# A ConvFFN down projection on one core: operand rests only on VectorE, in source order, with three more operand slots and paired steps

## The chip, the core and the metric

The kernel runs on one core of one Trainium2 chip. The metric is the device time of one execution in microseconds (us). TensorE (PE) does the matrix products, VectorE (DVE), ScalarE (ACT) and GpSimd (POOL) prepare operands and take results out of the banks, SyncE (SP) issues most transfers.

## What is computed

One layer of a hybrid block on 1024 tokens of width 1024: norm, three mixers, a residual, then a ConvFFN and a last norm. The change lies in the ConvFFN's last product; hidden width is 2816 = 22 x 128.

```python
def conv_ffn(u, w_up, conv_w, conv_b, w_down):
    hid = dwconv(u @ w_up, conv_w, conv_b, (1, 1))
    gate, val = jnp.split(hid, 2, axis=-1)
    return (jax.nn.silu(gate) * val) @ w_down
...
    h = h + mod[5] * conv_ffn(u, ffn_w_up[l], ffn_conv_w[l], ffn_conv_b[l], ffn_w_down[l])
  return rms_norm(h, final_g)
```

## The kernel before, in words

**Precision.** Every fp32 operand of a product is split into a rounded part and a rest (`split`, L214): ScalarE casts the source (L215), then the rest = source - rounded part is subtracted (L216), on VectorE or on GpSimd as the argument `lo` says. Three matmuls (high x high, low x high, high x low) make one product.

**Up projection (before L1927).** 22 pairs of blocks (gate and value) are made one after the other. `Pair.conv` (L1680) convolves one of the two along the tokens, `Pair.out` (L1701) convolves both, multiplies silu(gate) by the value and writes 512 KB to a buffer in HBM (`hid[i]`). The convolution of the last pair, i = 21, falls into the down projection.

**Down projection (L1927 to L2190).** A Strassen-like scheme with 2 x 2 blocks and seven products, run as four parts, each over 11 slices k of the hidden width (`K2 = 11`; slice k pairs the blocks k and k + 11):

- the alpha part (loop at L2091): two products, into four banks X and four banks Y. Its operands for slice k are two blocks of the weight (`wr`, one load of 512 KB per slice) and two of the hidden values (`hd`, two loads of 512 KB), made by `alpha_ops` (L2018). The sums of hidden blocks that the later parts need are made here by `sums_b` (L2022), three VectorE subtractions per slice, three slices behind (`LAG`).
- the beta part (L2114): its operands need more subtractions (`beta_ops`, L2032: L2035, L2037, L2039, and L2042 for the gamma part).
- the gamma part (L2129), and the delta part (L2175), whose operands are all made ahead.

A step (`step`, L1987) is one slice into one group of four banks: 4 x 3 = 12 matmuls of 128 x 512, at L1991 (high x high; the first argument is the stationary block), L1992 (its rest) and L1993 (the other operand's rest). Up to now every slice is one X step, then one Y step. Between two parts `add_to` (L1995, L1998) adds the banks to the residual on VectorE, four instructions per group.

**Operand slots.** An operand takes a slot of 128 x 1024 (`operand`, L1976). There are three with the tag `wh`, three with `wl`, and from the 13th operand on (`GV_AT = 12`) four with `gv`: 10 in all. A slot is free when the step that read its operand is done.

**Order.** PE's order is that of the source throughout. From L1927 to L2079 (`turn_order`) the other engines keep to the source too; behind L2079 a list scheduler orders VectorE, ScalarE and GpSimd by its own estimates. SP issues the loads in a queue: a `wr` load stands until one of two buffers is free, that is until both rests of the slice two before are done.

Of the kernel before, what the change touches and what calls it, by code (L numbers as in the profile page):

```python
# [9 lines left out]
F32R = mybir.dt.float32r  # L10
# [13 lines left out]
HID = 22  # L24
LAG = 3
LAG1 = 2
OUT_AT = 1
GV_AT = 12
HT_AT = 7
UP_DVE = (1, 4, 6)  # L30
# [78 lines left out]


def tile_kernel(tc, I, out, dbg=None):
    nc = tc.nc
    V, S, G, PE, SY = nc.vector, nc.scalar, nc.gpsimd, nc.tensor, nc.sync
    es = ExitStack()
    left = dict(side="left")
    right = dict(side="right")

    cst = es.enter_context(tc.tile_pool(name="cst", bufs=1, **left))
    wst = es.enter_context(tc.tile_pool(name="wst", bufs=1, **left))
# [6 lines left out]
    def nm(s):  # L126
        cnt[0] += 1
        return f"{s}{cnt[0]}"
# [4 lines left out]
    def t4(name="x", dt=F32):  # L133
        return px_.tile([128, 1024], dt, name=nm(name), tag="x", bufs=8)
# [4 lines left out]
    def pt(shape=(128, 512), dt=F32):  # L139
        return wst.tile(list(shape), dt, name=nm("pt"), tag="pt", bufs=2)  # L140
# [73 lines left out]
    def split(h, l, src, lo=G):  # L214
        S.copy(h, src)  # L215
        lo.tensor_tensor(l, src, f32(h), OP.subtract)  # L216
# [1331 lines left out]
    for m in range(KT):  # L1548
        w = wm.pop(0)
        p = mm()  # L1550
        tg = wide_in(tsp[m], "tg")
        for k in range(4):
            kk = slice(k * 128, (k + 1) * 128)
# [15 lines left out]
    pgv_ = pgv.__enter__()  # L1569
# [36 lines left out]
    def product(bk, w, b, first, ks=range(4)):  # L1606
        for k in ks:
            product_k(bk, w, b, first, k)

    class Pair:  # L1610
# [69 lines left out]
        def conv(self, b):  # L1680
# [17 lines left out]
                                       a[:, t0_ + c - 1:t0_ + n - 1], OP.mult, OP.add)  # L1698
            return a

        def out(self, queue=SY):  # L1701
            ga, va = self.conv(0), self.conv(1)
            S.activation(ga, ga, AF.Silu)
            V.tensor_tensor(ga, ga, va, OP.mult)
            queue.dma_start(hid[self.i], ga)

    q = [Pair(0), Pair(1)]
    accs = []
    for j in range(2):
        sl = tl[j]  # L1710
        acc = pt()
        for m in range(8):
            w = wm.pop(0)
# [3 lines left out]
            for k in range(KT):  # L1717
                kk = slice(k * 128, (k + 1) * 128)
# [40 lines left out]
    def bank(tag):  # L1759
        return pu_.tile([128, 512], F32, name=nm("bk" + tag), tag="bk" + tag, bufs=2)  # L1760
# [128 lines left out]
    norm_order.__exit__(None, None, None)  # L1889
    nxt.sums((7, 3))  # L1890
    q[0].p4()
    q[0].out()
    q[1].p3()
    q[1].p4()
    nxt.open("cd")
    for i in range(2, HID):
        pair, nxt = nxt, None
        if i > 2:
            pair.p1()
        pair.c1()  # L1900
        pair.load(5)
        if i > 2:
            pair.open()
            pair.p6()
        pair.z6()
        pair.load(7)
        product(pair.C, pair.w[5], T1, True)
        pair.load(2)
        product(pair.D, pair.w[7], T3, True)
        pair.z57()  # L1910
        pair.load(3, 4)
        if i + 1 == HID:
            break
        pair.p2()
        nxt = Pair(i + 1)
        nxt.fetch()
        nxt.sums()
        pair.p3()
        nxt.load(1, 6)
        if i == 2:  # L1920
            q[1].out()
        pair.p4()
        pair.out()

    turn_order = tc.manual_schedule(engines=ENGS - {mybir.EngineType.SP})  # L1927
# [10 lines left out]
    K2 = HID // 2  # L1938
    pdl = tc.tile_pool(name="pdl", bufs=1, **left, reuse_waits="tile")
    pdr = tc.tile_pool(name="pdr", bufs=1, **right, reuse_waits="tile")  # L1940
    pd = pdl.__enter__(), pdr.__enter__()
    home = {}
    for n in range(16):
        home["l", n] = 0
# [25 lines left out]
    def hid_load(k, queue=SY):  # L1970
        for i in (k, k + K2):
            queue.dma_start(raw[i], hid[i])

    ops_n = [0]

    def operand(src, lo=V):  # L1976

        c = ops_n[0] % 10 if ops_n[0] >= GV_AT else ops_n[0] % 2
        if c in (2, 5, 8, 9):
            w = pgv_.tile([128, 1024], F32R, name=nm("wp"), tag="gv", bufs=4)  # L1980
        else:
            w = wst.tile([128, 1024], F32R, name=nm("wp"), tag=("wh", "wl")[c % 2], bufs=3)
        ops_n[0] += 1
        split(w[:, 0:512], w[:, 512:1024], src, lo)
        return w

    def step(acc, w, b, first=False):  # L1987
        for m in range(4):
            mw = slice(m * 128, (m + 1) * 128)
            wh, wl = w[:, 0:512][:, mw], w[:, 512:1024][:, mw]  # L1990
            PE.matmul(acc[m], wh, b[:, 0:512], start=first, stop=False, skip_group_check=True)  # L1991
            PE.matmul(acc[m], wl, b[:, 0:512], start=False, stop=False, skip_group_check=True)  # L1992
            PE.matmul(acc[m], wh, b[:, 512:1024], start=False, stop=True, skip_group_check=True)  # L1993

    def add_to(r, c, acc):  # L1995
        for m in range(4):
            x = hT[4 * r + m][:, tl[c]]
            V.scalar_tensor_tensor(x, acc[m], md5[:, 4 * r + m:4 * r + m + 1], x, OP.mult, OP.add)  # L1998

    def b11(k):  # L2000
        return raw[k][:, tl[0]]

    def b12(k):
        return raw[k][:, tl[1]]

    def b21(k):
        return raw[k + K2][:, tl[0]]

    def b22(k):
        return raw[k + K2][:, tl[1]]  # L2010
# [4 lines left out]
    def alpha_load(k):  # L2015
        aw[k] = wraw(wd[k][:, 0:1024])

    def alpha_ops(k):  # L2018
        a12, a11 = (aw[k][:, t] for t in tl)
        return operand(a11, G), operand(b11(k)), operand(a12, G), operand(b21(k))  # L2020

    def sums_b(k):  # L2022
        V.tensor_tensor(b11(k), b12(k), b11(k), OP.subtract)
        V.tensor_tensor(spare[k], b22(k), b11(k), OP.subtract)
        V.tensor_tensor(b21(k), b21(k), spare[k], OP.subtract)

    def beta_load(k):
        a11 = tmp()
        SY.dma_start(a11, wd[k][:, 512:1024])
        aw[k] = a11, wraw(wd[k][:, 1024:2048])  # L2030

    def beta_ops(k):  # L2032
        a11, r = aw[k]
        a21, a22 = r[:, tl[0]], r[:, tl[1]]
        V.tensor_tensor(a22, a21, a22, OP.add)  # L2035
        t1 = operand(b11(k))
        V.tensor_tensor(b11(k), a11, a21, OP.subtract)  # L2037
        t2 = operand(spare[k])
        V.tensor_tensor(spare[k], a22, a11, OP.subtract)  # L2039
        s2 = operand(spare[k])  # L2040
        s1 = operand(a22)
        V.tensor_tensor(b12(k), b22(k), b12(k), OP.subtract)  # L2042
        return s2, t2, s1, t1

    def gamma_load(k):
        aw[k] = tmp()
        SY.dma_start(aw[k], wd[k][:, 0:512])

    def gamma_ops(k):
        s3, t3 = operand(b11(k)), operand(b12(k))  # L2050
        V.tensor_tensor(aw[k], aw[k], spare[k], OP.subtract)
        return s3, t3, operand(aw[k]), operand(b22(k))
# [21 lines left out]
    ops = [alpha_ops(0)]  # L2074
    V.tensor_tensor(pair.gv[0][:, tl[1]], pair.gv[1][:, tl[1]], pair.C, OP.add)
    X = [bank(t) for t in "abcd"]
    V.tensor_tensor(pair.gv[1][:, tl[1]], pair.gv[1][:, tl[1]], pair.D, OP.add)
    ops.append(alpha_ops(1))
    turn_order.__exit__(None, None, None)  # L2079
    hid_load(2)  # L2080
    alpha_load(2)
    hT = []
# [1 line left out]
    def h_loads(n):  # L2084
        if 0 <= n - HT_AT < 8:
            hx = t4("h")
            SY.dma_start(hx, hsp[n - HT_AT])
            hT.append(hx)

    Y = [bank(t) for t in "abcd"]  # L2090
    for k in range(K2):  # L2091
        if k + 3 < K2:
            if k + 3 < K2 - 1:
                hid_load(k + 3)
            alpha_load(k + 3)
        w1, o1, w2, o2 = ops.pop(0)
        step(X, w1, o1, k == 0)
        step(Y, w2, o2, k == 0)
        if k == OUT_AT:
            pair.out(S)  # L2100
        if k == OUT_AT + 2:
            hid_load(K2 - 1)
        h_loads(k)
        if k + 2 < K2:
            ops.append(alpha_ops(k + 2))
        elif k + 2 == K2:
            beta_load(0)
        if k >= LAG:
            sums_b(k - LAG)
    add_to(0, 0, X)  # L2110
    beta_load(1)
    ops = [beta_ops(k) for k in range(2)]
    add_to(0, 0, Y)
    for k in range(K2):  # L2114
        if k + LAG1 < K2 and k + LAG1 > K2 - 1 - LAG:
            sums_b(k + LAG1)
        w1, o1, w2, o2 = ops.pop(0)
        step(X, w1, o1)
        step(Y, w2, o2, k == 0)
        h_loads(K2 + k)  # L2120
        if k + 2 < K2:
            beta_load(k + 2)
            ops.append(beta_ops(k + 2))
        else:
            gamma_load(k + 2 - K2)
    add_to(0, 1, X)
    add_to(1, 1, Y)
    ops = [gamma_ops(k) for k in range(2)]
    for k in range(K2):  # L2129
        w1, o1, w2, o2 = ops.pop(0)  # L2130
        step(X, w1, o1)
        step(Y, w2, o2)
        if k + 2 < K2:
            gamma_load(k + 2)
            ops.append(gamma_ops(k + 2))
        if k % 2 == 0:
            delta_load(k)
        delta_ops(k)
    add_to(1, 1, X)
    add_to(0, 1, Y)  # L2140

# [30 lines left out]
    for c0, c1 in ((0, 256), (256, 512)):  # L2172
        for m in range(4):
            mw = slice(m * 128, (m + 1) * 128)
            for k in range(K2):  # L2175
                wh, wl = (w[:, mw] for w in dw[k])
# [11 lines left out]
    c0, c1 = pend[1]  # L2188
    last_out(c0, c1, norm_sums(pend[0], (c1 - c0) // 128, bank("a")))
    pe_order.__exit__(None, None, None)  # L2190
    pdr.__exit__(None, None, None)
    pgv.__exit__(None, None, None)
    px.__exit__(None, None, None)
# [98 lines left out]
```

## Time and profile before

| | |
|---|---|
| three runs | 1617.78, 1621.47 (median), 1622.53 us |
| profiled execution | 1620.94 us, span of the records 1619.1 us |
| PE busy | 1527.9 us, 94% of the span |
| VectorE busy | 1095.1 us, 68% |
| ScalarE busy | 770.0 us, 48% |
| GpSimd busy | 504.8 us, 31% |
| granted TensorE clock | mean 0.978 of full |

The page shows PE busy for nine tenths of the span: time can be gained there only by closing PE's gaps. The shares are means over all stages, so the rows below are taken from the stretch of the down projection, some 1365 to 1575 us from the span's start. A busy time counts a matmul from its start to a modelled end, so that neighbours overlap; the pace is read from the starts.

### The profile page before, as it was taken

How to read it: one execution, taken by the hardware profiler on the slowest of the kernel's cores; microseconds unless marked ns; L12 is line 12 of the kernel's file. 1: busy time of each engine (PE TensorE's matmuls, PEld its weight loads, DVE VectorE, ACT ScalarE, POOL GpSimd, SP SyncE). 2: the span in 40 equal slices, each digit the busy share in tenths (PEclk: the TensorE clock that was granted, in tenths of full speed). 3: DMA queues.
4: the chain of work that ended last, by engine and by line, in shares of the span. 5: the costliest groups of instructions: out<-in, count | busy, mean ns of one | idle time of the engine just before them, and what ended most of it. 6: DMA issues, size and time to landing. Idle time of an engine off the chain costs nothing. (4 is left out here: it accounts for less than half of the span.)

```text
span 1619.1 us, 21583 instructions
## 1 busy us (share of the span) xinstructions
PE 1527.9 (94%) x8144; PEld 1256.8 (78%) x8144; DVE 1095.1 (68%) x1598; ACT 770.0 (48%) x1221; POOL 504.8 (31%) x313
## 2 busy tenths in 40 slices
PE   5999999799998999999999998999999999789997
PEld 4888767677887788788888767878888888568887
DVE  4533569979877442642451799888888887898962
ACT  4424776665545544441333555444444444334661
POOL 3313233421113332222236444333333333630032
PEclk9999999899999999999999999999999999999998
DMA  9663623222214245132574411222222225664203
GB/s 347 236 220 98 223 84 115 95 86 66 68 53 131 94 124 157 54 88 72 170 233 141 142 41 62 81 80 101 80 78 79 79 88 202 223 247 156 98 20 105
DMA packets 93784, 198.91 MB, mean 123 GB/s; under 512 B 13488, under 2 KB 34864, under 8 KB 93552
## 3 DMA queue, kind: packets, MB, share of 16 engines
q1 hardware_dynamic: 81968, 181.62, 33.6%
q10 hardware_dynamic: 11712, 15.91, 2.8%
q8 instruction: 64, 1.05, 0.3%
q14 instruction: 40, 0.33, 0.1%
HBM read 158.98 MB, written 38.52 MB: 122 GB/s over the span
## 5 line engine op out<-in xcount | busy, mean ns | idle before, releaser
L216 POOL TENSOR_TENSOR wl<-wr,wh 128x1024 fp32r<-128x1024 f32 (+2 forms) x87 | 183.3, 2109 | 455.5 <-ACT wh L215 428.2
L215 ACT CAST wh<-wr 128x1024 fp32r<-128x1024 f32 (+2 forms) x87 | 77.3, 891 | 140.4 <-issue 42.0
L216 POOL TENSOR_TENSOR wp<-tmp,wp 128x512 fp32r<-128x512 f32 x44 | 73.9, 1698 | 221.5 <-ACT wp L215 221.5
L529 PE MATMUL ma<-uh,wh 128*128 128x512 f32 x272 | 117.4, 432 | 4.5 <-ACT pt L796 4.5
L529 PE MATMUL mb<-uh,wh 128*128 128x512 f32 x272 | 107.0, 394 | 0.0
L531 PE MATMUL ma<-ul,wh 128*128 128x512 f32 x272 | 107.0, 393 | 0.0
L531 PE MATMUL mb<-ul,wh 128*128 128x512 f32 x272 | 106.9, 393 | 0.0
L533 PE MATMUL mb<-uh,wl 128*128 128x512 f32 x272 | 106.6, 392 | 0.0
L533 PE MATMUL ma<-uh,wl 128*128 128x512 f32 x272 | 106.4, 391 | 0.0
L216 POOL TENSOR_TENSOR wp<-wr,wp 128x512 fp32r<-128x512 f32 x44 | 82.1, 1878 | 40.5 <-ACT wp L215 40.5
L215 ACT CAST wp<-tmp 128x512 fp32r<-128x512 f32 x78 | 46.5, 620 | 96.1 <-DVE tmp L1630 92.2
L1694 DVE SCALAR_TENSOR_TENSOR ca<-gv,vec,ca 128x1023 f32<-128x1023 f32 (+2 forms) x66 | 62.3, 968 | 24.4 <-ACT ca L1686 24.2
L215 ACT CAST wp<-hd 128x512 fp32r<-128x512 f32 x88 | 51.7, 618 | 55.1 <-PE bkd L1993 39.9
L215 ACT CAST wp<-wr 128x512 fp32r<-128x512 f32 x97 | 57.4, 620 | 42.5 <-DVE wr L2035 9.7
L1697 DVE SCALAR_TENSOR_TENSOR ca<-gv,vec,ca 128x1023 f32<-128x1023 f32 (+2 forms) x66 | 73.1, 1131 | 0.0
L216 DVE TENSOR_TENSOR wp<-hd,wp 128x512 fp32r<-128x512 f32 x88 | 61.4, 723 | 13.8 <-ACT wp L215 13.5
L529 PEld LDWEIGHTS ma<-uh,wh 128*128 128x128 f32 x272 | 51.7, 190 | 20.9 <-issue 6.7
L533 PEld LDWEIGHTS ma<-uh,wl 128*128 128x128 f32 x272 | 51.4, 189 | 11.5
L533 PEld LDWEIGHTS mb<-uh,wl 128*128 128x128 f32 x272 | 51.3, 189 | 11.4
L531 PEld LDWEIGHTS ma<-ul,wh 128*128 128x128 f32 x272 | 51.3, 189 | 11.3
L531 PEld LDWEIGHTS mb<-ul,wh 128*128 128x128 f32 x272 | 51.3, 189 | 11.3
L529 PEld LDWEIGHTS mb<-uh,wh 128*128 128x128 f32 x272 | 51.7, 190 | 9.7 <-issue 1.4
(628 smaller groups left out, 4634.2 us busy)
## 6 DMA issues: line engine op xcount, KB each, us to landing
wa<-in_ada_dram SPq DMA_DIRECT2D x96, 256.0 KB
wr<-in_wup_dram SPq DMA_DIRECT2D x46, 512.0 KB
wr<-in_win_dram SPq DMA_DIRECT2D x40, 512.0 KB
wr<-in_wdn_dram SPq DMA_DIRECT2D x22, 512.0 KB
hd<-hid SPq DMA_DIRECT2D x22, 512.0 KB
hid<-ca SPq DMA_DIRECT2D x21, 512.0 KB
wr<-in_wout_dram SPq DMA_DIRECT2D x16, 512.0 KB
tmp<-in_wdn_dram SPq DMA_DIRECT2D x22, 256.0 KB
```

Of the source, the lines that this page charges most:

```text
L215: S.copy(h, src)
L216: lo.tensor_tensor(l, src, f32(h), OP.subtract)
L529: PE.matmul(p[j], h[:, kk], uh[j][:, k], start=f, stop=False)
L531: PE.matmul(p[j], h[:, kk], ul[j][:, k], start=False, stop=False)
L533: PE.matmul(p[j], l[:, kk], uh[j][:, k], start=False, stop=e)
L1694: V.scalar_tensor_tensor(a[:, t0_ + 1:t0_ + 1 + n1], x[:, o:o + n1], fw[0], a[:, t0_ + 1:t0_ + 1 + n1], OP.mult, OP.add)
L1697: V.scalar_tensor_tensor(a[:, t0_ + c - 1:t0_ + n - 1], x[:, o + c:o + n], fw[2], a[:, t0_ + c - 1:t0_ + n - 1], OP.mult, OP.add)
```

## The change

It does five things, all in the down projection:

- `alpha_ops` makes its two weight operands' rests on VectorE instead of GpSimd (22 instructions).
- `turn_order` ends in the round k = 8 of the alpha loop instead of ahead of it, so that the engines follow the source that far; in the loop `sums_b` now stands ahead of `alpha_ops`.
- `Pair.out` no longer convolves the gate; a new `Pair.gate` does. For the last pair, `gate` stands in the round k = 0 and `out` in k = 1. For all other pairs `gate` stands directly ahead of `out`, which leaves their instructions in the same order.
- a third tag, `wz`, with three slots: 9 slots from the start and 13 from the 13th operand on, taken in a fixed rotation.
- PE's steps: the first two and the last two slices of a part go X, X, Y, Y instead of X, Y, X, Y (`steps`).

```diff
 class Pair:
+        def gate(self):
+            self.ga = self.conv(0)
+
         def out(self, queue=SY):
-            ga, va = self.conv(0), self.conv(1)
+            ga, va = self.ga, self.conv(1)
...
     def operand(src, lo=V):
-        c = ops_n[0] % 10 if ops_n[0] >= GV_AT else ops_n[0] % 2
-        if c in (2, 5, 8, 9):
-            w = pgv_.tile([128, 1024], F32R, name=nm("wp"), tag="gv", bufs=4)
-        else:
-            w = wst.tile([128, 1024], F32R, name=nm("wp"), tag=("wh", "wl")[c % 2], bufs=3)
+        c = ops_n[0] - GV_AT
+        tag = ("wh", "wl", "wz", "gv")[min(c % 13 % 4 if c % 13 < 12 else 3, 3)] if c >= 0 else ("wh", "wl", "wz")[c % 3]
+        w = {"gv": pgv_, "wz": pd[2]}.get(tag, wst).tile([128, 1024], F32R, name=nm("wp"), tag=tag,
+                                                        bufs=4 if tag == "gv" else 3)
...
     def alpha_ops(k):
-        return operand(a11, G), operand(b11(k)), operand(a12, G), operand(b21(k))
+        return operand(a11), operand(b11(k)), operand(a12), operand(b21(k))
...
     ops.append(alpha_ops(1))
-    turn_order.__exit__(None, None, None)
...
+    def steps(k, first_x, first_y):
+        def do(acc, kk, first):
+            w1, o1, w2, o2 = ops[kk]
+            step(acc, *((w1, o1) if acc is X else (w2, o2)), first)
+        if k in (0, K2 - 2):
+            for acc, f in ((X, first_x), (Y, first_y)):
+                do(acc, k, f and k == 0)
+                do(acc, k + 1, False)
+        elif k not in (1, K2 - 1):
+            do(X, k, False)
+            do(Y, k, False)
...
     for k in range(K2):
...
-        w1, o1, w2, o2 = ops.pop(0)
-        step(X, w1, o1, k == 0)
-        step(Y, w2, o2, k == 0)
-        if k == OUT_AT:
+        steps(k, True, True)
+        if k == 0:
+            pair.gate()
+        if k == 1:
             pair.out(S)
-        if k == OUT_AT + 2:
+        if k == 3:
             hid_load(K2 - 1)
         h_loads(k)
+        if k >= LAG:
+            sums_b(k - LAG)
         if k + 2 < K2:
             ops.append(alpha_ops(k + 2))
         elif k + 2 == K2:
             beta_load(0)
-        if k >= LAG:
-            sums_b(k - LAG)
+        if k + 2 == K2 - 1:
+            turn_order.__exit__(None, None, None)
```

**VectorE at the start of the alpha part, before.** `wp` is an operand, `hd` a hidden block, `wr` a weight block, `ca` the last convolution; L216 is a rest, L2023 to L2025 the sums:

```order
L216 TENSOR_TENSOR wp_11249<-hd_11225,wp_11249 128x512
L2023 TENSOR_TENSOR hd_11225<-hd_11225 128x512
L2024 TENSOR_TENSOR hd_11229<-hd_11226,hd_11225 128x512
L216 TENSOR_TENSOR wp_11255<-hd_11226,wp_11255 128x512
L2075 TENSOR_TENSOR gv_11102<-gv_11103,bkc_11109 128x512
L2025 TENSOR_TENSOR hd_11226<-hd_11226,hd_11229 128x512
L2077 TENSOR_TENSOR gv_11103<-gv_11103,bkd_11110 128x512
L216 TENSOR_TENSOR wp_11267<-hd_11235,wp_11267 128x512
L1694 SCALAR_TENSOR_TENSOR ca_11353<-gv_11102,vec,ca_11353 128x1023
L216 TENSOR_TENSOR wp_11273<-hd_11236,wp_11273 128x512
```

The same place in the changed kernel (a rest is now L215, and lines behind it are five further on):

```order
L215 TENSOR_TENSOR wp_11249<-wr_11243,wp_11249 128x512
L215 TENSOR_TENSOR wp_11252<-hd_11228,wp_11252 128x512
L215 TENSOR_TENSOR wp_11255<-wr_11243,wp_11255 128x512
L215 TENSOR_TENSOR wp_11258<-hd_11229,wp_11258 128x512
L2080 TENSOR_TENSOR gv_11102<-gv_11103,bkc_11109 128x512
L2082 TENSOR_TENSOR gv_11103<-gv_11103,bkd_11110 128x512
L215 TENSOR_TENSOR wp_11267<-wr_11247,wp_11267 128x512
L215 TENSOR_TENSOR wp_11270<-hd_11238,wp_11270 128x512
L215 TENSOR_TENSOR wp_11273<-wr_11247,wp_11273 128x512
L215 TENSOR_TENSOR wp_11276<-hd_11239,wp_11276 128x512
```

All four rests of a slice stand together, and the sums, which stood among them, come later: the first one stands 29 rows behind the first row shown here.

**GpSimd at the same place, before** (the first 5 of 22 such rows; the row ahead of them is the up projection's last):

```order
L216 TENSOR_TENSOR wp_11157<-pt_11041,wp_11157 128x512
L216 TENSOR_TENSOR wp_11246<-wr_11240,wp_11246 128x512
L216 TENSOR_TENSOR wp_11252<-wr_11240,wp_11252 128x512
L216 TENSOR_TENSOR wp_11264<-wr_11244,wp_11264 128x512
L216 TENSOR_TENSOR wp_11270<-wr_11244,wp_11270 128x512
```

And now, where what follows the up projection is the squares' sum of the last norm:

```order
L215 TENSOR_TENSOR wp_11139<-wr_11031,wp_11139 128x512
L215 TENSOR_TENSOR wp_11157<-pt_11041,wp_11157 128x512
L2178 TENSOR_TENSOR acc_12776<-acc_12776,tmp_12779 128x512
L2178 TENSOR_TENSOR acc_12776<-acc_12776,tmp_12783 128x512
L2178 TENSOR_TENSOR acc_12776<-acc_12776,tmp_12787 128x512
```

No GpSimd instruction is left between the up projection and the last norm.

**VectorE from the alpha part to the beta part, before** (`h` is the residual, `bka` to `bkd` the X banks; `wp_11756` is the weight operand of beta's first X step, `wp_11759` of its first Y step):

```order
L2035 TENSOR_TENSOR wr_11705<-wr_11705 128x512
L2037 TENSOR_TENSOR hd_11225<-tmp_11703,wr_11705 128x512
L2039 TENSOR_TENSOR hd_11229<-wr_11705,tmp_11703 128x512
L216 TENSOR_TENSOR wp_11759<-wr_11705,wp_11759 128x512
L1998 SCALAR_TENSOR_TENSOR h_11619<-bka_11259,md,h_11619 128x512
L1998 SCALAR_TENSOR_TENSOR h_11660<-bkb_11260,md,h_11660 128x512
L1998 SCALAR_TENSOR_TENSOR h_11701<-bkc_11261,md,h_11701 128x512
L1998 SCALAR_TENSOR_TENSOR h_11734<-bkd_11262,md,h_11734 128x512
L216 TENSOR_TENSOR wp_11756<-hd_11229,wp_11756 128x512
```

And now (numbers differ between the programs: `wp_11759` is here the weight operand of beta's first X step):

```order
L2040 TENSOR_TENSOR wr_11735<-wr_11735 128x512
L2003 SCALAR_TENSOR_TENSOR h_11621<-bka_11262,md,h_11621 128x512
L2003 SCALAR_TENSOR_TENSOR h_11662<-bkb_11263,md,h_11662 128x512
L2003 SCALAR_TENSOR_TENSOR h_11728<-bkc_11264,md,h_11728 128x512
L2003 SCALAR_TENSOR_TENSOR h_11737<-bkd_11265,md,h_11737 128x512
L2042 TENSOR_TENSOR hd_11228<-tmp_11733,wr_11735 128x512
L215 TENSOR_TENSOR wp_11755<-hd_11232,wp_11755 128x512
L215 TENSOR_TENSOR wp_11762<-wr_11735,wp_11762 128x512
L2044 TENSOR_TENSOR hd_11232<-wr_11735,tmp_11733 128x512
L2040 TENSOR_TENSOR wr_11748<-wr_11748 128x512
L215 TENSOR_TENSOR wp_11767<-hd_11238,wp_11767 128x512
L215 TENSOR_TENSOR wp_11759<-hd_11232,wp_11759 128x512
```

The four additions of the X banks now stand ahead of the subtractions (L2042, L2044) that beta's first X step needs.

## Rows read from the trace of the kernel before

**Rows 1.** Busy time by stage: alpha, beta, gamma, and beta and gamma without gaps.

```profile
core 0: us, PE busy (x) PEld busy (x) DVE busy (x) ACT busy (x) POOL busy (x), PEclk, DMA share, GB/s
1371.20:1445.60 74.40, 63.50 (x265) 50.46 (x264) 67.26 (x82) 28.36 (x49) 40.70 (x20) 0.95 0.67 242
...
1453.40:1571.40 118.00, 118.00 (x513) 96.04 (x513) 99.45 (x157) 64.52 (x113) 5.89 (x5) 1.00 0.30 99
```

**Rows 2.** Timeline of PE (start us, us; in brackets idle before and releaser).

```profile
1371.21 0.39 PE L1991 MATMUL bka<-wp,wp 128*128 128x512 f32 x1
...
1395.85 0.40 PE L1991 MATMUL bka<-wp,wp 128*128 128x512 f32 x1
...
1404.21 0.79 PE L1992 MATMUL bka<-wp,wp 128*128 128x512 f32 x1 [7.96 <-POOL wp L216]
1404.80 0.63 PE L1993 MATMUL bka<-wp,wp 128*128 128x512 f32 x1
...
1445.67 0.40 PE L1991 MATMUL bka<-wp,wp 128*128 128x512 f32 x1
1447.57 0.50 PE L1992 MATMUL bka<-wp,wp 128*128 128x512 f32 x1 [1.50 <-DVE wp L216]
...
1451.85 0.51 PE L1991 MATMUL bka<-wp,wp 128*128 128x512 f32 x1 [1.47 <-DVE h L1998]
...
1453.45 0.40 PE L1992 MATMUL bkb<-wp,wp 128*128 128x512 f32 x1
```

**Rows 3.** GpSimd: its rests in the alpha part, and its timeline at the longest.

```profile
L216 POOL TENSOR_TENSOR wp<-wr,wp 128x512 fp32r<-128x512 f32 x22 | 44.6, 2050 | 35.6 <-ACT wp L215 35.6
...
1391.92 15.94 POOL L216 TENSOR_TENSOR wp<-wr,wp 128x512 fp32r<-128x512 f32 x4 [4.43 <-ACT wp L215]
```

**Rows 4.** What SP's queue waited for, 1355 to 1480 us (us in total, times, longest).

```profile
SPq L206 <- POOL wp L216: 51.8, 10, 16.5
```

**Rows 5.** Transfers in stretches of 5 us, and over 1360 to 1440 us (columns as in rows 1).

```profile
1370.00:1375.00 5.00, 5.00 (x23) 4.12 (x23) 4.91 (x7) 1.44 (x3) 1.89 (x3) 1.00 1.03 415
...
1400.00:1405.00 5.00, 0.79 (x2) 0.70 (x3) 3.03 (x6) 0.00 (x0) 5.00 (x2) 0.62 0.00 0
...
DMA packets 5848, 21.37 MB, mean 267 GB/s; under 512 B 640, under 2 KB 640, under 8 KB 5844
```

**Rows 6.** Timeline of VectorE (first and last rows of stretches).

```profile
1368.04 0.88 DVE L216 TENSOR_TENSOR wp<-hd,wp 128x512 fp32r<-128x512 f32 x1 [3.43 <-ACT wp L215]
...
1384.57 1.78 DVE L2023 TENSOR_TENSOR hd<-hd 128x512 f32<-128x512 f32 x1
...
1390.31 0.68 DVE L2023 TENSOR_TENSOR hd<-hd 128x512 f32<-128x512 f32 x1
1390.91 0.68 DVE L2025 TENSOR_TENSOR hd<-hd,hd 128x512 f32<-128x512 f32 x1
...
1444.21 0.73 DVE L1998 SCALAR_TENSOR_TENSOR h<-bka,md,h 128x512 f32<-128x512 f32 x1
1444.87 0.73 DVE L1998 SCALAR_TENSOR_TENSOR h<-bkb,md,h 128x512 f32<-128x512 f32 x1
```

**Rows 7.** VectorE's groups with shapes: two of 1365 to 1440 us, then 1455 to 1500 us.

```profile
L2023 DVE TENSOR_TENSOR hd<-hd 128x512 f32<-128x512 f32 x11 | 11.7, 1070 | 0.1
L1697 DVE SCALAR_TENSOR_TENSOR ca<-gv,vec,ca 128x1023 f32<-128x1023 f32 x1 | 1.3, 1273 | 0.0
...
L216 DVE TENSOR_TENSOR wp<-hd,wp 128x512 fp32r<-128x512 f32 x27 | 17.8, 682 | 2.6 <-ACT wp L215 2.6
L216 DVE TENSOR_TENSOR wp<-wr,wp 128x512 fp32r<-128x512 f32 x9 | 6.2, 684 | 1.5 <-ACT wp L215 1.5
```

**Rows 8.** ScalarE's timeline: a cast, and the last pair's write on its queue.

```profile
1367.39 0.62 ACT L215 CAST wp<-hd 128x512 fp32r<-128x512 f32 x1 [0.40 <-DMA hd<-hid]
...
1389.81 0.33 ACTq L1705 DMA_DIRECT2D hid<-ca  x1
1390.18 1.14 ACT L215 CAST wp<-hd 128x512 fp32r<-128x512 f32 x2 [6.19 <-DVE ca L1704]
```

More of the change, by code (lines that the diff above doesn't have):

```diff
@@ L26 @@
 LAG1 = 2
-OUT_AT = 1
 GV_AT = 12
@@ L1891, in tile_kernel @@
     q[0].p4()
+    q[0].gate()
     q[0].out()
@@ L1920, in tile_kernel @@
         if i == 2:
+            q[1].gate()
             q[1].out()
         pair.p4()
+        pair.gate()
         pair.out()
@@ L1940, in tile_kernel @@
     pdr = tc.tile_pool(name="pdr", bufs=1, **right, reuse_waits="tile")
-    pd = pdl.__enter__(), pdr.__enter__()
+    pdz = tc.tile_pool(name="pdz", bufs=1, **right, reuse_waits="tile")
+    pd = pdl.__enter__(), pdr.__enter__(), pdz.__enter__()
     home = {}
@@ L2095, in tile_kernel @@
             alpha_load(k + 3)
-        w1, o1, w2, o2 = ops.pop(0)
-        step(X, w1, o1, k == 0)
-        step(Y, w2, o2, k == 0)
-        if k == OUT_AT:
+        steps(k, True, True)
+        if k == 0:
+            pair.gate()
+        if k == 1:
             pair.out(S)
-        if k == OUT_AT + 2:
+        if k == 3:
             hid_load(K2 - 1)
         h_loads(k)
+        if k >= LAG:
+            sums_b(k - LAG)
         if k + 2 < K2:
@@ L2116, in tile_kernel @@
             sums_b(k + LAG1)
-        w1, o1, w2, o2 = ops.pop(0)
-        step(X, w1, o1)
-        step(Y, w2, o2, k == 0)
+        steps(k, False, True)
         h_loads(K2 + k)
@@ L2129, in tile_kernel @@
     for k in range(K2):
-        w1, o1, w2, o2 = ops.pop(0)
-        step(X, w1, o1)
-        step(Y, w2, o2)
+        steps(k, False, False)
         if k + 2 < K2:
@@ L2190, in tile_kernel @@
     pe_order.__exit__(None, None, None)
+    pdz.__exit__(None, None, None)
     pdr.__exit__(None, None, None)
```

## The prediction

> **What bounds the kernel now.** I read the page first (PE is busy for 94% of the span, so only gaps of PE can give time), then the busy times by stage, PE's timeline in the down projection, and for each gap the timeline of the engine that ended it.
>
> By stage [rows 1]: from 1453.40 to 1571.40 us, PE starts 513 matmuls in 118.0 us and has no gap, 0.230 us each. From 1371.20 to 1445.60 us, the alpha part, it is busy for 63.50 of 74.40 us, at a granted clock of 0.95. Alpha has 11 slices x 24 = 264 matmuls, which at 0.230 us are 60.7 us. PE's timeline [rows 2] has the alpha part from 1371.21 to 1445.67 = 74.5 us: 13.7 us are lost. From there to the fifth matmul of beta's first Y step at 1453.45 are 16 matmuls, 3.7 us of work in 7.8 us: 4.1 us more are lost. Sum 17.8 us. Behind it, to the delta part, there is nothing to gain.
>
> The largest gap [rows 2] runs from 1395.85 to 1404.21, 8.4 us for one matmul, and was ended by a rest on GpSimd. The next seven matmuls start some 0.43 us apart instead of 0.23, and the granted clock of that stretch is 0.62 [rows 5]: PE, idle for 8 us, came back at about the lower level of 1.2 GHz. GpSimd's rests [rows 3] take 2.05 us in the mean, and four of them took 15.94 us from 1391.92 on. VectorE then ran subtractions back to back, 0.60 us from start to start [rows 6]. Where GpSimd got through, VectorE's same instruction took 1.78 us [rows 6]. So each holds the other up. SP's queue waited 51.8 us in all for GpSimd's rests before it could issue a weight load [rows 4], and hidden blocks stand behind those loads in the queue: from 1400 to 1405 us no byte moved [rows 5]. At the change from alpha to beta PE waited for a rest on VectorE (1.50 us) and then for the Y banks' additions (1.47 us) [rows 2].
>
> **The change, part by part.**
>
> *Rests off GpSimd.* 22 rests go; 22 come to VectorE at 0.602 us each, 13.2 us. From start to start a VectorE subtraction takes 0.60 us where GpSimd is idle; the groups of 1455 to 1500 us have 0.68 us as the mean of one, of which 0.08 overlaps the next [rows 6, 7]. But the order also moves work out: beta's early subtractions and seven of the eleven L2042 now stand in the beta part. From the first rest to the one ahead of the X additions VectorE has 83 rows: 76 subtractions or additions of 512 columns (45.8 us), two convolution instructions of 1023 columns (1.2 each, from 1.27 less the overlap [rows 7]), four halves at 0.66 (as rows of that kind take against the banks [rows 6]) and a product of 1024 columns (1.1): 52 us. They start at 1367 [rows 6, 8] and could end at 1419. PE has work until 1371.2 + 60.7 = 1431.9. They fit, so the 13.7 us of alpha can go, the clock's part among them.
>
> The Trainium skill (Perfetto Trace Analysis, section Optimizing Scalar/DVE Operations) says that if VectorE is saturated, moving work to ScalarE or even GpSimd may make sense, and that with the shared read port it may not help; this edit goes the other way with VectorE busy 67.26 of 74.40 us [rows 1]. By the first half of that rule the sum would be 67.26 + 13.2 = 80.5 us for alpha, 6 us slower than now. I don't take it, since the 67.26 us hold the instructions of 1.78 us beside GpSimd [rows 6], and since 82 VectorE instructions became about 77 in that stretch.
>
> *Paired steps at alpha's start.* X of slice 1 is due at 1371.2 + 2.76 = 1374.0, one step earlier than now. Its rests follow the addition of bank d (bank ready at 1371.4): 1372.0, 1372.6, 1373.2. It fits by 0.8 us. The last operand of slice 2 takes a slot that the first Y step frees, now at 1379.5; its rest ends at 1380.9 and is due at 1385.0.
>
> *Convolution in two pieces.* The same instructions. The write of the last pair's result stands on ScalarE's queue [rows 8] and holds the casts behind it until VectorE's product is done, as it did (6.19 us). Now the four casts of slice 3 stand behind it too. Product done 1384.8, casts at 0.52 us, the rests that the X step needs at 1387.0, and that step is due at 1387.8: nothing lost, with 0.8 us to spare. The load of that block stands behind three more weight loads in SP's queue, a wait of no cost.
>
> *Three more slots.* A slot comes back after 13 operands instead of 10. No instruction; the waits of the casts for PE's steps get shorter. Cost nothing, and below nothing only through the terms above.
>
> *Alpha to beta.* X is complete two steps before alpha's end, at 1426.4. Four additions at 0.66 us [rows 6] end at 1429.1; then four instructions to L2044, 1431.5; the cast of 0.62 us [rows 8], 1432.1; two more and the rest, at 1433.4. PE is ready at 1431.9 and loses 1.25 us. For the X step of slice 1: L2044 of that slice at 1435.7, then two additions of Y stand ahead of its rest, which ends at 1437.7 against a due time of 1436.2: 1.5 us lost. Y's additions are done at 1438.9, ahead of the Y step at 1440.2. So 2.8 us replace the 4.1.
>
> *Beta.* VectorE now has 100 rows here, against some 85: 92 x 0.602 + 8 x 0.66 = 60.7 us, as much as PE's 60.7. From 1438.9 there are 80 rows to the rest that the X step of slice 10 needs: 48.2 us, 1487.1. Paired, that step is due at 1431.9 + 2.8 + 19 x 2.76 = 1487.2. It fits to the tenth only if VectorE never waits. In 1455 to 1500 us it waited for casts for 2.6 + 1.5 us [rows 7], at most 5 us with small ones. So the cost lies between 0 and 5 us. I take 1.0: those waits came while VectorE was ahead of PE and cost nothing, and there are more slots now.
>
> *Gamma and delta.* PE had no gap there [rows 1]. VectorE has 7 instructions per slice, 4.2 us for PE's 5.5; additions come two steps before the end. Nothing.
>
> **Sum.** 17.8 - 2.8 - 1.0 = 14.0 us. The profiled execution took 1620.94 us (span 1619.1), 0.5 below the median of the three runs, 1621.47. Forecast: 1620.9 - 14.0 = 1606.9 us. With every gap closed it would be 1603.1.
>
> **The rivals.**
>
> *VectorE sets beta's pace.* If it waits for casts as often as in 1455 to 1500 us, the X step of slice 10 comes 5.4 us late instead of 1.0: 1611.3 us. For: 100 rows of beta fill PE's time exactly. Against: at those waits it had run ahead.
>
> *The transfers set alpha's pace.* From 1360 to 1440 us 21.37 MB moved at a mean of 267 GB/s [rows 5]. If that were the most they give, the loads would take the same 80 us and PE would wait for hidden blocks instead: 1621 us, no change. Against: 415 GB/s from 1370 to 1375 us, and 0 from 1400 to 1405, when the queue stood for GpSimd [rows 4, 5]. 31 loads of 0.52 MB from 1361.6 to 1422 need 270 GB/s.
>
> *VectorE stays slow with GpSimd idle: slower than before.* Were its subtractions slow for another reason, the 76 of alpha would run at the mean of the sums there, 1.07 us, or 0.99 from start to start [rows 7]: with the convolution at its slow pace 86 us from 1367, so the last X step starts at 1450 instead of 1423.6. That is 26 us lost where 13.7 were: with beta's 3.8 us about 1633 us. It decides from 0.88 us from start to start on; below that the change still gains. The rule of the Trainium skill above (Perfetto Trace Analysis, section Optimizing Scalar/DVE Operations) would point the same way. For: VectorE was busy for 90% of alpha. Against: 0.60 us in all rows without a GpSimd instruction getting through [rows 6, 7], also from 1441 to 1455 us.
>
> *The change doesn't do what it says.* The order keeps the source only to the eighth round, and sums of slices 6 and 7 are drawn ahead of the rests by up to six rows, 3.6 us. The rests there are due some 4 us later, so I count it in no case.
>
> **How the numbers follow.** The forecast, 1603 to 1610 us, has 0.72; VectorE in beta 0.15; the transfers 0.08; slow VectorE 0.05. A measurement can tell about 0.3% (4.9 us) from no change. The first two are faster by more: 0.87. The third is the same: 0.08. The last is slower: 0.05. The range takes the first two, with their bounds and half a microsecond at the low end for the runs' spread: 1602.5 to 1613.0.
>
> **What would show it.** Right: alpha from its first to beta's first matmul in 61 to 62 us at a clock of 1.00, no GpSimd row between the up projection and the last norm, no VectorE subtraction of 1.78 us there, weight loads issued without long waits, two gaps of 1 to 2 us at beta's start. Wrong: a gap at slice 2 or 3 (pairing, or the write on ScalarE's queue), casts ended by transfers (second rival), PE gaps at beta's end ended by VectorE's rests (first), subtractions over 0.8 us (third).

## The result and the profile after

Five runs of the changed kernel took 1601.49 to 1605.79 us, median 1604.05; five of the kernel before in the same comparison 1617.78 to 1622.53, median 1620.83. The ratio is 0.9896 [0.9882, 0.991]: 16.8 us less, faster by more than the 0.3% that can be told. The profiled execution took 1601.49 us, with a span of 1599.7 us.

The lines of code have moved by a few numbers: rests are L215, matmuls L1996 to L1998, additions L2003, `sums_b` L2028 to L2030, `beta_ops` L2040 to L2047.

The busy times by stage, with the columns of [rows 1] (alpha, beta, gamma):

```profile
1371.20:1432.00 60.80, 60.80 (x266) 49.59 (x265) 57.28 (x91) 28.21 (x50) 0.00 (x0) 1.00 0.88 321
1432.00:1497.00 65.00, 64.22 (x279) 51.75 (x278) 64.69 (x107) 30.54 (x53) 0.00 (x0) 1.00 0.40 130
1497.00:1556.00 59.00, 59.00 (x271) 48.71 (x270) 47.65 (x72) 39.32 (x70) 10.49 (x8) 1.00 0.18 58
```

PE is busy for all of alpha, at a granted clock of 1.00 in place of 0.95. GpSimd does nothing, and VectorE, which took over 22 rests, is busy for 57.28 us in the stretch, where it was busy for 67.26 before. The transfers moved 321 GB/s where they had moved 242.

PE's timeline holds alpha's end and the only gap of the two parts:

```profile
1421.88 0.39 PE L1996 MATMUL bka<-wp,wp 128*128 128x512 f32 x1
1422.11 0.39 PE L1997 MATMUL bka<-wp,wp 128*128 128x512 f32 x1
1422.33 0.39 PE L1998 MATMUL bka<-wp,wp 128*128 128x512 f32 x1
...
1430.05 0.40 PE L1996 MATMUL bka<-wp,wp 128*128 128x512 f32 x1
...
1432.88 0.49 PE L1996 MATMUL bka<-wp,wp 128*128 128x512 f32 x1
1434.15 0.50 PE L1997 MATMUL bka<-wp,wp 128*128 128x512 f32 x1 [0.78 <-DVE wp L215]
...
1552.85 1.34 PE L2195 MATMUL bka<-hd,hd 128*128 128x256 f32 x10
```

Alpha's first matmul starts at 1369.30, beta's at 1430.05: 60.75 us for 264 matmuls. The second X step of beta waits about 1.0 us for a rest. From alpha's first matmul to the first of the delta part (1552.85) it is 183.55 us; before, from 1371.21 to 1571.48, 200.27. So 16.7 us came from this stretch; the other 2.7 of the 19.4 us between the two spans lie in code that is the same. This stretch is the sharper measure, and is given for each run below.

VectorE's groups with shapes, 1365 to 1450 us (compare [rows 7]), and what SP's queue waited for, 1355 to 1480 us (compare [rows 4]):

```profile
L215 DVE TENSOR_TENSOR wp<-hd,wp 128x512 fp32r<-128x512 f32 x38 | 25.6, 686 | 0.5 <-ACT wp L214 0.5
L215 DVE TENSOR_TENSOR wp<-wr,wp 128x512 fp32r<-128x512 f32 x27 | 18.5, 686 | 4.8 <-ACT wp L214 4.8
...
L2028 DVE TENSOR_TENSOR hd<-hd 128x512 f32<-128x512 f32 x8 | 5.3, 686 | 0.0
```

```profile
SPq L205 <- DVE wp L215: 49.7, 18, 7.3
```

No subtraction takes longer than 0.69 us in the mean; the L2023 of [rows 7], 1.07 us then, is L2028 now. SP's queue still waits for 49.7 us in all for VectorE's rests, but in 18 waits of at most 7.3 us, where one of 16.5 us was among the ten for GpSimd's.

### The profile page after: what moved, and what is told of

The parts are those of the page before. It is cut to its first block, busy times and chain, and to the rows that moved or that the text cites. A ratio compares the mean times of both kernels' runs of the same rounds, so it can differ in the third digit from the quotient of the medians.

```text
span 1599.7 us, 21566 instructions
## 1 busy us (share of the span) xinstructions
PE 1521.8 (95%) x8144; PEld 1254.7 (78%) x8144; DVE 1092.8 (68%) x1620; ACT 770.1 (48%) x1221; POOL 461.3 (29%) x291
## 3 DMA queue, kind: packets, MB, share of 16 engines
q8 instruction: 64, 1.05, 0.3%
## 5 line engine op out<-in xcount | busy, mean ns | idle before, releaser
L215 POOL TENSOR_TENSOR wl<-wr,wh 128x1024 fp32r<-128x1024 f32 (+2 forms) x87 | 183.4, 2109 | 455.7 <-ACT wh L214 428.5
L215 POOL TENSOR_TENSOR wp<-tmp,wp 128x512 fp32r<-128x512 f32 x44 | 74.1, 1701 | 220.4 <-ACT wp L214 203.4
L1693 DVE SCALAR_TENSOR_TENSOR ca<-gv,vec,ca 128x1023 f32<-128x1023 f32 (+2 forms) x66 | 61.4, 954 | 23.7 <-ACT ca L1685 23.6
L214 ACT CAST wp<-wr 128x512 fp32r<-128x512 f32 x97 | 58.2, 620 | 36.4 <-DMA wr<-in_wdn_dram 17.4
L1696 DVE SCALAR_TENSOR_TENSOR ca<-gv,vec,ca 128x1023 f32<-128x1023 f32 (+2 forms) x66 | 70.6, 1093 | 0.1
L2178 POOL TENSOR_TENSOR acc<-acc,tmp 128x256 f32<-128x256 f32 (+1 forms) x9 | 9.0, 1002 | 182.8 <-ACT tmp L2175 182.7
L215 DVE TENSOR_TENSOR wp<-hd,wp 128x512 fp32r<-128x512 f32 x88 | 60.7, 708 | 1.3 <-ACT wp L214 1.1
```

The source lines that it names most:

```text
L1693: V.scalar_tensor_tensor(a[:, t0_ + 1:t0_ + 1 + n1], x[:, o:o + n1], fw[0], a[:, t0_ + 1:t0_ + 1 + n1], OP.mult, OP.add)
L1696: V.scalar_tensor_tensor(a[:, t0_ + c - 1:t0_ + n - 1], x[:, o + c:o + n], fw[2], a[:, t0_ + c - 1:t0_ + n - 1], OP.mult, OP.add)
```

## The experiments

Each kernel ran beside the kernel before on the same chip. "Stretch" is the time from alpha's first to delta's first matmul in the profiled run.

| run | median us | ratio to before | stretch us |
|---|---|---|---|
| before | 1620.83 | 1 | 200.27 |
| changed | 1604.05 | 0.9896 [0.9882, 0.991] | 183.55 |
| e1 rests alone | 1602.69 | 0.9899 [0.9882, 0.9916] | 183.50 |
| e2 rests back | 1613.39 | 0.9965 [0.9954, 0.9975] | 196.13 |
| e3 ten slots | 1603.98 | 0.9902 [0.9885, 0.9918] | 184.65 |
| e4 unpaired | 1601.67 | 0.9891 [0.9873, 0.9909] | 182.79 |
| e5 scheduler | 1602.98 | 0.9885 [0.987, 0.9899] | 182.17 |
| e6 idle GpSimd | 1614.89 | 0.9956 [0.9942, 0.997] | 194.37 |
| e7 more VectorE | 1619.52 | 0.999 [0.9979, 1.0001] | 200.30 |
| e8 beta first | 1608.34 | 0.9916 [0.9902, 0.993] | 188.86 |
| e9 one input | 1604.99 | 0.9904 [0.9888, 0.992] | 186.59 |
| e10 ScalarE | 1607.62 | 0.9918 [0.9903, 0.9934] | 185.01 |
| e11 writes, elsewhere | 1608.98 | 0.9922 [0.9907, 0.9938] | 184.16 |
| e12 writes in place | 1605.46 | 0.9901 [0.9881, 0.992] | 183.59 |

**e1: the rests alone**, in the kernel before.

```diff
-        return operand(a11, G), operand(b11(k)), operand(a12, G), operand(b21(k))
+        return operand(a11), operand(b11(k)), operand(a12), operand(b21(k))
```

> The kernel before with the 22 weight rests of the alpha part on VectorE and nothing else: scheduler's order, ten slots, unpaired steps. My theory (GpSimd's slow rests and the hold-up between the two engines make nearly all of alpha's 13.7 us): alpha loses at most 4 us, the 4.1 us at its end stay, time 1607 to 1611 us. Rival (the order and the slots matter as much, the rests only change their place): alpha still loses 8 us or more, time 1615 us or more.

It took 1602.69 us, stretch 183.50: the whole gain of the change by one line, and less than the 1607 to 1611 us that I had given. I had thought that the 4.1 us lost behind alpha would stay; 1.2 are left. PE's timeline has two gaps, both at the start of beta's first Y step and ended by additions:

```profile
1435.44 0.50 PE L1991 MATMUL bka<-wp,wp 128*128 128x512 f32 x1 [0.58 <-DVE h L1998]
1436.70 0.50 PE L1991 MATMUL bkb<-wp,wp 128*128 128x512 f32 x1 [0.30 <-DVE h L1998]
```

**e2: the rests back on GpSimd**, in the changed kernel (the edit of e1 the other way).

> The changed kernel with the 22 rests back on GpSimd; order, slots and paired steps stay. My theory: alpha loses 8 us or more again, now with all of a slice's rests on GpSimd due in turn, time 1612 to 1622 us. Rival (order and slots carry the gain): time at most 1608 us.

The median is 1613.39 us, the stretch 12.6 us longer than the changed kernel's. GpSimd's group and VectorE's, 1365 to 1450 us, and PE's longest gap:

```profile
L215 POOL TENSOR_TENSOR wp<-wr,wp 128x512 fp32r<-128x512 f32 x22 | 48.5, 2229 | 33.7 <-ACT wp L214 33.7
```

```profile
L215 DVE TENSOR_TENSOR wp<-hd,wp 128x512 fp32r<-128x512 f32 x30 | 31.5, 1079 | 4.7 <-ACT wp L214 4.7
...
L2028 DVE TENSOR_TENSOR hd<-hd 128x512 f32<-128x512 f32 x9 | 9.4, 1048 | 0.0
```

```profile
1415.32 0.79 PE L1998 MATMUL bka<-wp,wp 128*128 128x512 f32 x1 [6.91 <-DVE wp L215]
1415.92 0.63 PE L1996 MATMUL bkb<-wp,wp 128*128 128x512 f32 x1
```

VectorE has 22 instructions fewer and is late nonetheless: these two groups take 1.08 and 1.05 us in the mean again, and PE's longest gap is ended by a rest of VectorE's, not of GpSimd's. Such a mean mixes two kinds of rows: in e2 as in the kernel before, nearly every subtraction of 512 columns takes either 0.67 to 0.69 us or some 1.78. The stretch is 4.1 us shorter than in the kernel before, so order, slots and pairing together are worth about that much while GpSimd has the rests; without them there e1 shows no worth of these parts.

**e3, e4, e5: one other part undone**, in the changed kernel: the ten slots and rotation of before; every slice as X, Y; the source order ending ahead of the alpha loop.

```diff
-        c = ops_n[0] - GV_AT
...
+        c = ops_n[0] % 10 if ops_n[0] >= GV_AT else ops_n[0] % 2
```

> The changed kernel with the ten operand slots of before. My theory (slots cost nothing as long as VectorE has room): within 2 us of the changed kernel, 1603 to 1606 us, except that the paired steps at alpha's start have two operands fewer in advance, at most 3 us. Rival (slots are what lets VectorE run ahead in beta, where it has as much work as PE): PE gaps in beta, 1608 us or more.

```diff
-        if k in (0, K2 - 2):
-            for acc, f in ((X, first_x), (Y, first_y)):
-                do(acc, k, f and k == 0)
-                do(acc, k + 1, False)
...
+        do(X, k, first_x and k == 0)
+        do(Y, k, first_y and k == 0)
```

> The changed kernel with X and Y steps in turn throughout. My theory (pairing gives VectorE time for the X banks' additions at a change of parts): the gaps at beta's start grow from 1.2 to 4 or 5 us, time 1606 to 1609 us; nothing at gamma's start. Rival (pairing gives nothing, the gain is all in alpha): 1603 to 1605 us.

```diff
     ops.append(alpha_ops(1))
+    turn_order.__exit__(None, None, None)
...
-        if k + 2 == K2 - 1:
-            turn_order.__exit__(None, None, None)
```

> The changed kernel with the source order ended where it ended before, so that the scheduler orders VectorE, ScalarE and GpSimd in the alpha part; rests on VectorE, 13 slots and paired steps stay. My theory (VectorE has room in alpha, so the order of its rows costs little): within 3 us of the changed kernel, at most 1607 us. Rival (sums ahead of rests are what makes PE wait): 1609 us or more, with PE gaps in alpha ended by VectorE's rests.

None differs from the changed kernel by more than its interval: 1603.98, 1601.67 and 1602.98 us. In e4, where I had counted on gaps of 4 or 5 us at the change of parts, the largest gap ahead of the delta part is 0.3 us more than a matmul's pace:

```profile
1432.40 0.50 PE L1996 MATMUL bkc<-wp,wp 128*128 128x512 f32 x1 [0.15 <-DVE h L2003]
```

With VectorE at 0.60 us from start to start, the additions of X and Y fit between the steps in either order. The pairing had nothing to repair.

**e6: idle work on GpSimd.** All rests stay on VectorE; GpSimd makes 36 subtractions that nobody reads, four in each of nine slices.

```diff
+    xa, xb = (pd[2].tile([128, 256], F32, name="xtr%d" % i, tag="xtr%d" % i, bufs=1) for i in range(2))
+    S.copy(xa, pair.gv[1][:, 0:256])
...
+        for _ in range(4 if k + 2 < K2 else 0):
+            G.tensor_tensor(xb, xa, xa, OP.subtract)
         if k + 2 < K2:
             ops.append(alpha_ops(k + 2))
```

> The changed kernel with four subtractions of 256 columns per alpha slice on GpSimd that nobody reads (36 in all). Tells the hold-up between the engines from the wait for GpSimd's results. My theory (each holds the other up): VectorE's rests beside them last 1.2 us or more in places and VectorE loses 5 to 15 us of its room in alpha; PE feels it once the room of some 8 us is gone: 1604 to 1612 us. Rival (only the wait for GpSimd's results cost time): no VectorE subtraction over 0.8 us, 1604 us.

The median is 1614.89 us, the stretch 10.8 us longer: more than I had allowed for. Nobody waits for these results, so the loss comes from the hold-up of VectorE alone. GpSimd's timeline, then VectorE's as GpSimd ends at 1408.02:

```profile
1394.83 13.19 POOL L2127 TENSOR_TENSOR xtr<-xtr 128x256 f32<-128x256 f32 x13
```

```profile
1405.43 1.10 DVE L2047 TENSOR_TENSOR hd<-hd,hd 128x512 f32<-128x512 f32 x1
1406.45 1.10 DVE L2030 TENSOR_TENSOR hd<-hd,hd 128x512 f32<-128x512 f32 x1
1407.47 1.09 DVE L215 TENSOR_TENSOR wp<-wr,wp 128x512 fp32r<-128x512 f32 x1
1408.49 0.68 DVE L215 TENSOR_TENSOR wp<-hd,wp 128x512 fp32r<-128x512 f32 x1
1409.09 0.68 DVE L215 TENSOR_TENSOR wp<-wr,wp 128x512 fp32r<-128x512 f32 x1
```

The same instruction takes 1.10 us beside GpSimd (1.02 from start to start) and 0.68 (0.60) behind it. GpSimd's 13 subtractions take 13.19 us, 1.01 each: here the two engines go by turns, one instruction each. An estimate of the loss: GpSimd was busy for 35.1 us, and 34 VectorE instructions at 0.42 us more are 14.4 us. In the changed kernel's alpha VectorE was idle for 60.80 - 57.28 = 3.5 us, which leaves 10.9 us; measured 10.8. That it fits so well is partly luck: some 8.5 of the 10.8 us are longer waits of PE's, and 2.3 are matmuls that start further apart behind them, which the estimate leaves out.

**e7: more work for VectorE.** The same 36 subtractions, on VectorE (`V` for `G`).

> The changed kernel with four subtractions of 256 columns per alpha slice more on VectorE that nobody reads (36 in all, some 0.33 us each, 12 us). My theory (VectorE has 52 us of work in alpha and must be done some 57 us after its start): about 7 us lost, less what its rows behind the rests can give, 1607 to 1612 us. Rival (VectorE has far more room than its busy time shows, since rests run slices ahead): 1604 to 1605 us.

It took 1619.52 us, the stretch 16.8 us longer, and I had expected 1607 to 1612. From start to start one takes 0.34 us, 12.2 in all; with the same 3.5 us idle, 8.7 should be lost. PE's longest gap and what follows it:

```profile
1439.25 0.80 PE L1997 MATMUL bka<-wp,wp 128*128 128x512 f32 x1 [3.79 <-DVE wp L215]
1439.85 0.79 PE L1998 MATMUL bka<-wp,wp 128*128 128x512 f32 x1
1440.44 0.63 PE L1996 MATMUL bkb<-wp,wp 128*128 128x512 f32 x1
1440.87 0.63 PE L1997 MATMUL bkb<-wp,wp 128*128 128x512 f32 x1
1441.30 0.63 PE L1998 MATMUL bkb<-wp,wp 128*128 128x512 f32 x1
```

There are five such gaps ahead of 1440, 10.6 us in all beyond the pace, and behind three of them PE starts matmuls every 0.43 us in place of 0.23: the other 6 us. The granted clock from 1439.25 to 1444 us is 0.50, the lower level. I had not priced that.

**e8: another order for beta's start.** What the first X steps read is drawn ahead, partly ahead of X's additions; the subtractions b11 and b12 go behind Y's (DVE and ACT in a written order).

```diff
-    add_to(0, 0, X)
...
-    ops = [beta_ops(k) for k in range(2)]
+    a22(0)
+    t2 = [operand(spare[0])]
+    t3_(0)
+    t2.append(operand(spare[1]))
+    add_to(0, 0, X)
+    s2 = [operand(spare[0])]
...
     add_to(0, 0, Y)
+    for k in range(2):
+        b11_(k)
+        V.tensor_tensor(b12(k), b22(k), b12(k), OP.subtract)
```

> The changed kernel with VectorE's and ScalarE's rows at beta's start in an order written out: what the first two X steps need stands ahead of the Y banks' additions and of the operands of the Y steps. My theory: the gap of 1.0 us at beta's second X step goes, no new one comes, about 1603 us, too little to tell from the changed kernel by the time alone. Rival (a cast or a load comes too late in the new order): a gap of 1 us or more at beta's start, 1604 us or more.

It was worse, as the rival had it: 1608.34 us, the stretch 5.3 us longer. The gap at beta's second X step is gone, but the X step of the third slice waits, and VectorE ahead of it for a weight load:

```profile
1445.13 0.50 PE L1996 MATMUL bka<-wp,wp 128*128 128x512 f32 x1 [1.43 <-ACT wp L214]
1447.45 0.80 PE L1997 MATMUL bka<-wp,wp 128*128 128x512 f32 x1 [1.82 <-DVE wp L215]
```

```profile
1446.11 0.69 DVE L2040 TENSOR_TENSOR wr<-wr 128x512 f32<-128x512 f32 x1 [1.07 <-DMA wr<-in_wdn_dram]
```

What I moved behind the additions reads the buffers that the next loads need. That this is why the load came late is read from the code and the wait, and was not tried apart.

**e9: one input instead of two.** e6 with copies on GpSimd.

```diff
-            G.tensor_tensor(xb, xa, xa, OP.subtract)
+            G.tensor_copy(xb, xa)
```

> The 36 idle GpSimd subtractions of the run with idle GpSimd work become copies with one input, of the same 128 x 256 elements. There a VectorE subtraction took 1.10 us beside GpSimd and 0.68 us alone. Theory (any GpSimd read beside a two-input VectorE operation holds it up): VectorE's subtractions beside the copies again take over 0.9 us, and the time lies over the changed kernel's 1604 by some part of those 11 us, 1607 to 1614, by how long the copies take. Rival (only GpSimd's own two-input operations do it): VectorE's subtractions stay at 0.68 us and the time is 1602 to 1605.

The median, 1604.99 us, is below the range that I gave the theory and inside the rival's; the trace decides. GpSimd's copies, and VectorE as they end at 1399.98:

```profile
1370.33 29.65 POOL L2127 COPY xtr<-xtr 128x256 f32<-128x256 f32 x36 [16.91 <-ACT xtr L2109]
```

```profile
1398.83 0.88 DVE L2047 TENSOR_TENSOR hd<-hd,hd 128x512 f32<-128x512 f32 x1
1399.63 0.88 DVE L2030 TENSOR_TENSOR hd<-hd,hd 128x512 f32<-128x512 f32 x1
1400.44 0.68 DVE L215 TENSOR_TENSOR wp<-wr,wp 128x512 fp32r<-128x512 f32 x1
```

One input holds VectorE up too, by 0.20 us from start to start (0.80 against 0.60), half of what two do: 27.5 us of copies beside 34 instructions are 6.9 us, less the 3.5 idle 3.4. The stretch is 3.0 us longer. My bound of 0.9 us for one subtraction was a hair too high, and I had not taken the idle time off.

**e11 and e12: writes only.** e11 puts 12 fills per slice in the same place; e12 ties them to the slice.

```diff
             ops.append(alpha_ops(k + 2))
+            S.copy(xb[:, 0:1], b21(k + 2)[:, 0:1])
+            for _ in range(12):
+                G.memset(xb, 0.0)
```

> GpSimd only writes: 108 fills of 128 x 256 with a constant in the same nine places, nothing read. Theory (the hold-up is between GpSimd's reads and VectorE's second input): VectorE's subtractions stay at 0.68 us and the time is that of the changed kernel, 1602 to 1606. Rival (any busy GpSimd slows VectorE, or writes do): VectorE's subtractions beside the fills take over 0.9 us and the time is 1608 to 1616.

e11 told nothing on this: with nothing to wait for, the fills ran at 767 to 814 us, in another stage. Its time, 1608.98, is no verdict on either theory.

> In the run with GpSimd's fills nothing held them back, and they ran at 767 to 814 us, in an earlier stage; so that run said nothing on the alpha part. Here a ScalarE copy of one column into the filled tile, behind each slice's casts, ties 12 fills (0.31 us each there, 3.7 us a slice, some 33 us in all) to each of nine slices of the alpha part. Theory (the hold-up is between GpSimd's reads and VectorE's second input): VectorE's subtractions beside the fills stay at 0.68 us, and the alpha part to the delta part stays at the changed kernel's 183.6 us within 1.5, the time 1602 to 1607. Rival (any busy GpSimd slows VectorE): the subtractions take over 0.85 us and that stretch is 187 us or more, the time 1607 to 1615.

e12's fills stand in alpha (GpSimd's timeline and VectorE's):

```profile
1399.73 4.38 POOL L2130 MEMSET xtr<- 128x256 f32 x12 [0.28 <-ACT xtr L2128]
```

```profile
1399.95 0.68 DVE L2028 TENSOR_TENSOR hd<-hd 128x512 f32<-128x512 f32 x1
1400.67 0.69 DVE L2029 TENSOR_TENSOR hd<-hd,hd 128x512 f32<-128x512 f32 x1
1401.28 0.69 DVE L2047 TENSOR_TENSOR hd<-hd,hd 128x512 f32<-128x512 f32 x1
```

VectorE keeps its pace, and the stretch is 183.59 us against 183.55. 33.7 us of GpSimd writing cost nothing; 27.5 us of copying cost 3.0, 35.1 us of subtracting 10.8.

The Trainium skill (SBUF — State Buffer, section Who interferes with whom) states that a VectorE instruction with two inputs in the on-chip memory (SBUF) contends with a GpSimd instruction that reads it, and not with one that only writes. e6, e9 and e12 agree: 1.02, 0.80 and 0.60 us from start to start.

**e10: the control.** The 36 copies on ScalarE (`S.copy`).

> The control: the same 36 idle operations of 128 x 256 as copies on ScalarE, whose busy time in the alpha part was 28.2 of 60.8 us. Theory (the hold-up belongs to GpSimd beside VectorE, not to more traffic in the on-chip memory): VectorE's subtractions stay at 0.68 us and, with some 13 us more for ScalarE, which casts wait for, the time is 1602 to 1607. Rival (any further reading and writing slows VectorE): its subtractions lengthen and the time is 1609 to 1616.

VectorE's subtractions stay at 0.68 to 0.69 us beside 14.7 us of copies, so reading and writing more is not what slows it (ScalarE's timeline, then VectorE's):

```profile
1401.82 1.73 ACT L2127 COPY xtr<-xtr 128x256 f32<-128x256 f32 x4
```

```profile
1402.10 0.68 DVE L215 TENSOR_TENSOR wp<-wr,wp 128x512 fp32r<-128x512 f32 x1
1402.70 0.68 DVE L215 TENSOR_TENSOR wp<-hd,wp 128x512 fp32r<-128x512 f32 x1
```

The median, 1607.62 us, lies 0.6 above the range: the stretch is 1.5 us longer, mostly by two gaps at 1488 us where no copy stands, and alpha begins 4 us later.

## Why the prediction was right

The forecast was 1606.9 us (1602.5 to 1613.0), the median is 1604.05. The likeliest case came true: all of alpha's lost time went.

- *Rests off GpSimd: 13.7 us.* Right, and it is all of the gain: e1 has it with this edit alone. The reason was that each engine holds the other up. e6, where GpSimd's work is read by nobody, shows one direction, VectorE slowed by GpSimd. With the change VectorE's mean durations fell from 1.07 us [rows 7] to 0.69. The other direction no run tried apart, but the trace of the kernel before has it, and there it ended the longest gap: of the four rests in 15.94 us [rows 3] one took 12.23 us, beside VectorE's subtractions at 0.60 us from start to start, and the other three 3.74 us, while VectorE stood still. PE waited 8.0 us for the first:

```profile
1391.92 12.23 POOL L216 TENSOR_TENSOR wp<-wr,wp 128x512 fp32r<-128x512 f32 x1 [4.43 <-ACT wp L215]
...
1404.11 3.74 POOL L216 TENSOR_TENSOR wp<-wr,wp 128x512 fp32r<-128x512 f32 x3
```

  That VectorE's instructions would go down to about 77 was wrong: it did 91 in alpha's 60.80 us, and they fitted.
- *Paired start, convolution in two pieces, slots: 0.* Right: alpha has no gap. The 0.8 us to spare that I had worked out at slices 1 and 3 were enough.
- *Alpha to beta: 2.8 us lost.* This term was mis-sized; the loss is 1.0. "X is complete two steps before alpha's end, at 1426.4" was the step that failed: the additions go bank by bank, and bank a is complete with the third of the step's twelve matmuls. VectorE's timeline has the additions four matmuls after the step's start at 1421.88, so they were done 1.7 us sooner after alpha's start than I had them, and the first X step waited for nothing; the second waited 1.0 us for the rest at 1433.41, behind two additions of Y, where I had 1.5:

```profile
1422.76 0.75 DVE L2003 SCALAR_TENSOR_TENSOR h<-bka,md,h 128x512 f32<-128x512 f32 x1 [0.85 <-PE bka L1998]
...
1432.75 0.74 DVE L2003 SCALAR_TENSOR_TENSOR h<-bkb,md,h 128x512 f32<-128x512 f32 x1
1433.41 0.68 DVE L215 TENSOR_TENSOR wp<-hd,wp 128x512 fp32r<-128x512 f32 x1
```

  Nor is what was gained here owed to the pairing and the new order: e1, with neither, loses 1.2 us, and e4, without the pairing, 0.3.

- *Beta: 1.0 us (0 to 5).* 0. VectorE, busy for 64.69 of 65.00 us there, never waited long: it ran at 0.60 us with casts ready ahead. The first rival falls with it, but e10 shows that the room is small: its two gaps at 1488 us, 1.9 us beyond the pace, stand at the X step of slice 10, which that rival named.
- *Gamma and delta: 0.* Right.
- *The sum.* 16.7 us in this stretch where I had 14.0: 1.8 us more by alpha to beta and 1.0 by beta.
- *Transfers as alpha's bound.* No: 321 GB/s in alpha, with PE never waiting. In the 5 us stretches of 1365 to 1385 us they gave 378 to 419. One sign of this rival did come: from 1365 to 1432 us ScalarE's casts waited seven times for a weight load, 17.4 us in all, at most 4.4. How much nearer alpha can come to this bound was not tried.
- *VectorE stays slow.* No: 0.68 us. The rule weighed with it (the Trainium skill, Perfetto Trace Analysis, section Optimizing Scalar/DVE Operations), that a saturated VectorE may give work away even to GpSimd, pointed the wrong way in its first half, which alone was weighed: VectorE gave less time to more work once GpSimd was idle. Its second half, that with the shared read port this may not help, agrees with these runs.
- *The change doesn't do what it says.* The order beyond the eighth round cost nothing, and e5 shows that it did nothing either.

No version here beats the changed kernel by more than can be measured; e1 equals it with a one-line edit. In the changed kernel's stretch one gap of 1.0 us is left.

## What to carry to other kernels

Before VectorE's busy time is taken as a load, its mean duration for one shape is read with and without GpSimd beside it: an engine that looks saturated may be held up by the work that was given away. A helper engine's instruction costs what it takes from the other one, here 0.20 us for each input of 256 columns that GpSimd read beside a two-input subtraction. The helper can be held up as well: 12.23 us for a subtraction that took 1.25 us with VectorE idle. When one engine feeds PE and has only 3.5 us to spare in 60, what is added beyond those was lost on PE (e6, e7, e9), and behind gaps of 2.8 us PE's clock was lower as well.

## What was not expected of the hardware

- Where the engines go by turns, VectorE is held up the more the more GpSimd reads: not by fills, 0.20 us by copies and 0.42 by subtractions of 256 columns, for each VectorE instruction. In the kernel before instructions took 1.78 us [rows 6] beside subtractions of 512 columns: some 1.1 us more from start to start, where 0.20 for each 256 columns read would make 0.8. Why it is more stays open.
- Beside VectorE's back-to-back subtractions one of GpSimd's took 12.23 us in the kernel before and ended at 1404.15, 1.1 us after VectorE's last; VectorE was not held up in that time. In e2 another took 14.61 us in the same way. When the engines go by turns and when one shuts the other out stays open.
- Behind gaps of 2.8 us (e7) PE came back at 0.43 us from matmul to matmul, as behind the 8.4 us of [rows 2]; behind 1.4 us (e7) and 2.1 us (e6) it did not.
- Alpha begins at 1367.2 (e4) to 1376.7 us (e11) from the span's start, though the code ahead of it is nearly the same. In e11 the fills stand ahead of it; for e12 (1375.2) the cause stays open. So differences of 2 to 4 us between medians here are not put down to the down projection without the stretch.
